# Two-layer hybrid encoder on one core: the products of probabilities and values in two matmuls a block, and one evacuation for two heads

## The chip, the core and the metric

The kernel runs on one core of one Trainium2 chip. The metric is the device time of one execution in microseconds (us). It is compared by the median of several runs; one further execution is taken with the hardware profiler, and its page and trace are what this document reads. Engines are named as in the profile: PE is TensorE (matmuls; PEld are its weight loads), DVE is VectorE, ACT is ScalarE, POOL is GpSimd, and SP issues transfers.

## The reference, cut to what matters

Two layers over 2048 tokens of width 1024. In each layer the normalised input goes through one wide projection; its columns feed a chunked attention (8 heads of 64) and a retention (4 heads of 128); both are gated, joined and projected back onto the input. The change touches the last step of the attention:

```python
def hybrid_layer(x, norm_gain, w_in, w_out, rel_bias, cos, sin):
    hn = rms_norm(x, norm_gain)
    aq, ak, av, ag, rq, rk, rv, rg = jnp.split(hn @ w_in, cuts, axis=-1)
    ya = chunked_rel_attention(aq, ak, av, rel_bias)      # softmax(q k / 8 + bias) v, own chunk + 8 before
    yr = chunkwise_retention(rq, rk, rv, cos, sin)
    y = jnp.concatenate([ya * silu(ag), yr * silu(rg)], axis=-1)
    return x + y @ w_out
```

For each token and head, `ya` is the sum over up to 576 keys of probability times value, where the probabilities are exponentials divided by their sum.

## The kernel before, in words

**Numbers in two halves.** Wherever precision matters, a float32 array is held as two float16 arrays, an upper half (the rounded value) and a lower half (what is left). A product then takes three matmuls: upper by upper, upper by lower, lower by upper.

**Tiles and stages.** Tokens go in 16 tiles of 128, four tiles to a block of 512 (n = 0 to 3). For each layer l and each of four groups s (two attention heads and one retention head), and for each block n, `dense_T` makes queries and keys, `dense_V` makes values and gates, and `attention` runs on the block. The main loop interleaves them: `run` takes one *round* of the dense work (eight matmuls of 512 columns), then lets the deferred work that has come due be issued (`tick`; `later(k, fn)` means: k rounds from now), then takes one step of the attention of the block before. One attention of a block has 24 rounds, six for each tile. After the last group comes `wout`, the projection back.

**Order.** PE, ACT, DVE and POOL issue their instructions in the order in which the program is written; an engine that waits holds up everything behind it on the same engine. SP's transfers have an order of their own except for those marked `in_turn`.

**Attention of a unit** (one tile a, one head hx; L830 to L882). `qk` makes the scores S in PSUM (L845, L846), VectorE adds the bias and takes the maximum (L849, L851), ScalarE makes the exponentials (L852) and their upper half (L854), GpSimd the lower half (L855), and a transposing transfer (L857) puts keys on the partitions: `u.p[:, b]` is the upper and `u.p[:, nb + b]` the lower half of block b of 128 keys, with nb up to 5 blocks. Two units later `pv` (L860) multiplies with the values. The values lie as `st.v[:, a, hx, 0:129]`: 64 columns upper half, one column of ones (L789), and 64 columns lower half (L811). Before, `pv` takes a PSUM bank for each unit and issues three matmuls a block: upper probabilities by upper values and ones (65 columns, L865), upper probabilities by lower values (64 columns, L866, added into the same columns 0 to 63), lower probabilities by upper values and ones (65 columns, L867). Column 64 is the sum of the probabilities. One round later `out_` (L869) takes its reciprocal (L871), multiplies it with the group's scale `g.ka` (L872) and scales the 64 columns with it and with the gate (L877). When both heads of a tile are there, y goes out to memory (L880). With rounds counted in a tile from 0: the first head's `pv` is in round 0, its `out_` at the tick of round 1, the second head's `pv` in round 3 and its `out_` at the tick of round 4.

**Retention** (L909). For each tile, a product r1 in round 0 (L916, masked at L918), and a product r2 in round 5 (L928, L931), evacuated by L939, L951 and L956; `sh` (L907) is the state's half for the next tile.

**PSUM.** Eight banks. Two (psD) hold the dense sums, two (psS) the scores, and four (psR, tag "small") everything else: the unit's o, r1, r2, and the sums of squares of weights that are being prepared (`allsum`, L334). A psR bank that has become free is given to the next taker in the order of last uses in the program.

Of the kernel before, what the change touches and what calls it, by code (L numbers as in the profile page):

```python
# [10 lines left out]
F32 = mybir.dt.float32  # L11
I32 = mybir.dt.int32
AF = mybir.ActivationFunctionType
ALU = mybir.AluOpType
# [4 lines left out]
P = 128  # L19
# [8 lines left out]
def hybrid_trunk(ctx: ExitStack, tc: tile.TileContext, x, pos, gain, gcol, w_in, w_out, rel, fgain,  # L28
# [8 lines left out]
    act, dve, pool, pe, sp = nc.scalar, nc.vector, nc.gpsimd, nc.tensor, nc.sync  # L37
# [5 lines left out]
    b2 = ctx.enter_context(tc.tile_pool(name="b2", bufs=2))  # L43
# [7 lines left out]
    psR = ctx.enter_context(tc.tile_pool(name="psR", bufs=4, space=PSUM))  # L51
# [16 lines left out]
    y_d = [dp.tile([P, D], F32, tag=f"y_d{t}", name=f"y_d{t}") for t in range(NT)]  # L68
# [554 lines left out]
    def in_turn(i):  # L623

        if not ring.get("free"):
            return
        tc.keep_in_program_order(i)


    def flow(k=0):  # L630

        if len(pipe) > k:
            pipe.pop(0)()
# [3 lines left out]
    def later(k, fn):  # L637
        deferred.append([k, fn])
# [184 lines left out]
    def attention(l, s, n, g, st, prev):  # L823
        units = []
        for a in range(4):
            for hx in range(2):
                units.append((a, hx))
        ya = {}

        def qk(a, hx):  # L830

            u = St()
            u.a, u.hx = a, hx
            u.nm = f"{l}_{s}_{n}_{a}_{hx}"
            u.nb = nb = min(5, 4 * n + a + 1)
            u.w = w = nb * P
            u.kts = [(st if t // 4 == n else prev, t % 4) for t in range(4 * n + a + 1 - nb, 4 * n + a + 1)]
            S = psS.tile([P, 1024], F32, tag="S", name=f"S{u.nm}")
            cs = slice(a * P, (a + 1) * P)
            cuts = sorted({0, nb} | {j for j in range(nb) if u.kts[j] == (st, 0) or j == 4})  # L840
            for j0, j1 in zip(cuts, cuts[1:]):
                q_, a_ = u.kts[j0]
                k_ = q_.k[:, hx, a_ * P:(a_ + j1 - j0) * P]
                o = S[:, j0 * P:j1 * P]
                pe.matmul(o, st.q[:, hx, 0, cs], k_, start=True, stop=False)  # L845
                pe.matmul(o, st.q[:, hx, 1, cs], k_, start=False, stop=True)  # L846
            v = b2.tile([P, 640], F32, tag="sc", name=f"sc{u.nm}")[:, 0:w]
            m = b2.tile([P, 1], F32, tag="mq", name=f"mq{u.nm}")
            dve.tensor_tensor_reduce(out=v, in0=S[:, 0:w], in1=g.bias[hx][:, 640 - w:640], scale=1.0, scalar=-3.0e38,  # L849
                                     op0=ALU.add, op1=ALU.max, accum_out=m)  # L850
            dve.tensor_scalar(m, m, g.nc[:, 0:1], LN_PSC, op0=ALU.mult, op1=ALU.add)  # L851
            act.activation(v, v, AF.Exp, bias=m[:, 0:1], scale=g.c[:, 0:1])  # L852
            pq = b2.tile([P, 1280], F16, tag="pq", name=f"pq{u.nm}")
            act.activation(pq[:, 0:w], v, AF.Copy)  # L854
            pool.tensor_tensor(pq[:, w:2 * w], v, pq[:, 0:w], op=ALU.subtract)  # L855
            u.p = b2.tile([P, 10, P], F16, tag="pT", name=f"pT{u.nm}")[:, 0:2 * nb, :]
            later(1, lambda: sp.dma_start_transpose(out=u.p, in_=pq[:, 0:2 * w]))  # L857
            return u

        def pv(u):  # L860
            t = 4 * n + u.a
            o = psR.tile([P, 512], F32, tag="small", name=f"o{u.nm}")
            for b, (q_, a_) in enumerate(u.kts):
                v_ = q_.v[:, a_, u.hx, :]
                pe.matmul(o[:, 0:65], u.p[:, b, :], v_[:, 0:65], start=(b == 0), stop=False)  # L865
                pe.matmul(o[:, 0:64], u.p[:, b, :], v_[:, 65:129], start=False, stop=False)  # L866
                pe.matmul(o[:, 0:65], u.p[:, u.nb + b, :], v_[:, 0:65], start=False, stop=(b == u.nb - 1))  # L867

            def out_():  # L869
                rl = b2.tile([P, 1], F32, tag="rl", name=f"rl{u.nm}")  # L870
                dve.reciprocal(rl, o[:, 64:65])  # L871
                dve.tensor_tensor(rl, rl, g.ka, op=ALU.mult)  # L872
                if u.hx == 0:
                    ya[u.a] = b2.tile([P, P], F32, tag="ya", name=f"ya{u.nm}")
                y = ya[u.a]
                vs = slice(u.hx * 64, u.hx * 64 + 64)
                dve.scalar_tensor_tensor(out=y[:, vs], in0=o[:, 0:64], scalar=rl[:, 0:1], in1=st.g[u.a][:, vs],  # L877
                                         op0=ALU.mult, op1=ALU.mult)
                if u.hx == 1:
                    later(1, lambda: in_turn(sp.dma_start(y_d[t][:, s * P:(s + 1) * P], y)))  # L880

            later(1, out_)  # L882

        ret = retention(l, s, n, g, st)
        rounds_ret = (5, 10, 10, 14, 14, 18, 18, 23) if (l, s, n) == (0, 0, 0) else [6 * a + b for a in range(4) for b in (0, 5)]
        for i, (a, hx) in enumerate(units):
            flow(1)
            u = qk(a, hx)
            for r in range(3 * i, 3 * i + 3):
                for _ in range(rounds_ret.count(r)):  # L890
                    next(ret, None)
                if r % 3 == 2:
                    pipe.append(lambda u=u: pv(u))
                yield
# [319 lines left out]
    def grp(l, s):  # L1214
        if (l, s) not in groups:
            groups[l, s] = Grp()
        return groups[l, s]
# [138 lines left out]
    for j in range(4):  # L1356
        o = VSEC[j] * 512
# [80 lines left out]
    for l in range(DEPTH):  # L1438
        gO = [Grp(), Grp()]
        go = Grp()  # L1440
        for s in range(NSW):
            g = grp(l, s)
            for n in range(NS):
                first = (l, s, n) == (0, 0, 0)
                if not first:
                    st = St()
                    states[l, s, n] = st
                    dT = dense_T(l, s, n, g, st)
                else:
                    st = st0  # L1450
# [129 lines left out]
```

## Time and profile before

| what | before |
|---|---|
| median of 3 runs | 2061.82 us (2058.64 to 2061.86) |
| span of the profiled execution, first to last instruction | 2060.7 us |
| mean granted clock of TensorE | 0.995 |
| ACT busy | 1134.8 us, 55% |
| POOL busy | 688.1 us, 33% |
| instructions | 39339 |

The profiled execution's time is its span and the little that lies before the first and behind the last instruction; the median run is 1.1 us above that span. How to read a row of the groups: line, engine, operation, output<-inputs by the program's names, shapes and count; then the busy time and the mean of one in nanoseconds; then the time that the engine sat idle right before them, and what ended most of it. A row of the timeline is start, duration, engine, line, operation and count; in brackets stands the idle time before it and what released it. In a row of the windows each engine has its busy time and, in parentheses, its instructions. Matmuls overlap one another, so their durations add up to more than the time they take.

### The profile page before, as it was taken

To read this page: it belongs to the slowest core of one execution; us is meant where nothing else is said; L and a number is where in the kernel's file an instruction comes from. 1 tells how busy PE (TensorE), PEld (TensorE's weight loads), DVE (VectorE), ACT (ScalarE), POOL (GpSimd) and SP (SyncE) were. 2 spreads that over 40 slices of the span, in tenths; PEclk is the share of its full clock that TensorE was granted. 3 is DMA by queue.
4 is the path that set the end of the run, shared out by engine and by line. 5 is a ranking of instruction groups with operands and counts; after the bars stand their busy time and mean duration, and the time that the engine had idled before them with its cause. 6 is when DMAs were issued, how large, how long until landed. Compare 5 with 4: busy or idle time off the path is not lost. (4 is left out here: it accounts for less than half of the span.)

```text
span 2060.7 us, 39339 instructions
## 1 busy us (share of the span) xinstructions
PE 1999.4 (97%) x14038; PEld 1052.9 (51%) x14038; DVE 1228.1 (60%) x3804; ACT 1134.8 (55%) x2526; POOL 688.1 (33%) x701
## 2 busy tenths in 40 slices
PE   6988999999999999999999999999999999999998
PEld 4444555555555555554444555555555555555544
DVE  6776666565556555666553556555655566557643
ACT  6556665556565645555444546655656565455432
POOL 0344343434334434430003443444333334333100
PEclk9999999999999999999999999999999999999999
DMA  8778664547584754899774546554746775658864
GB/s 227 169 161 178 155 148 109 112 114 164 117 185 113 165 128 101 174 209 263 219 185 113 124 104 156 116 126 103 158 117 150 148 155 124 129 115 187 224 203 139
DMA packets 645701, 313.64 MB, mean 152 GB/s; under 512 B 459232, under 2 KB 602080, under 8 KB 645504
## 3 DMA queue, kind: packets, MB, share of 16 engines
q1 hardware_dynamic: 645504, 311.12, 65.6%
q8 instruction: 110, 1.80, 0.4%
q14 instruction: 87, 0.71, 0.1%
HBM read 123.26 MB, written 41.98 MB: 80 GB/s over the span
## 5 line engine op out<-in xcount | busy, mean ns | idle before, releaser
L855 POOL TENSOR_TENSOR pq<-sc,pq 128x640 f16<-128x640 f32 (+4 forms) x256 | 319.4, 1248 | 860.5 <-ACT pq L854 443.8
L852 ACT ACTIVATE sc<-sc,mq,cT 128x640 f32<-128x640 f32 (+4 forms) x256 | 218.4, 853 | 615.6 <-DVE rl L871 309.7
L797 PE MATMUL dV<-whV,hTh 128*128 128x512 f16 x1024 | 353.9, 381 | 7.3 <-DVE gt L815 6.1
L797 PE MATMUL dV<-whV,hTl 128*128 128x512 f16 x1024 | 353.8, 381 | 0.0
L797 PE MATMUL dV<-wlV,hTh 128*128 128x512 f16 x1024 | 353.8, 381 | 0.0
L778 PE MATMUL dT<-hTh,whT 128*128 128x512 f16 x1008 | 346.6, 379 | 2.7 <-DVE kk L697 1.3
L778 PE MATMUL dT<-hTl,whT 128*128 128x512 f16 x1008 | 346.6, 379 | 0.0
L778 PE MATMUL dT<-hTh,wlT 128*128 128x512 f16 x1008 | 346.6, 379 | 0.0
L797 PEld LDWEIGHTS <-hTh 128*128 128x128 f16 x2048 | 197.0, 98 | 224.7 <-DVE gt L815 10.0
L778 PEld LDWEIGHTS <-whT 128*128 128x128 f16 x2016 | 192.1, 98 | 207.7 <-issue 1.6
L849 DVE CUSTOM_DVE_ANT_0 sc<-S,bias 128x640 f32<-128x640 f32 (+4 forms) x256 | 188.3, 735 | 88.8 <-PE S L846 87.4
L1172 PE MATMUL dO<-whO,yly 128*128 128x512 f16 x504 | 191.0, 379 | 1.7 <-DMA yly<-hTl 1.1
L1172 PE MATMUL dO<-whO,yhy 128*128 128x512 f16 x504 | 191.0, 379 | 1.0 <-DMA yhy<-hTh 1.0
L1172 PE MATMUL dO<-wlO,yhy 128*128 128x512 f16 x504 | 191.0, 379 | 0.0
L854 ACT ACTIVATE pq<-sc 128x640 f16<-128x640 f32 (+4 forms) x256 | 171.5, 670 | 8.1
L797 PEld LDWEIGHTS <-hTl 128*128 128x128 f16 x1024 | 99.4, 98 | 112.4 <-issue 3.9
L1172 PEld LDWEIGHTS <-yhy 128*128 128x128 f16 x1008 | 98.1, 98 | 113.7 <-DMA yhy<-hTh 1.5
L778 PEld LDWEIGHTS <-wlT 128*128 128x128 f16 x1008 | 97.2, 98 | 113.7 <-issue 6.0
L845 PE MATMUL S<-k,q 128*128 128x128 f16 (+3 forms) x592 | 142.4, 267 | 0.0
L865 PE MATMUL o<-v,pT 128*128 128x65 f16 x1120 | 129.8, 193 | 6.4 <-DMA pT<-pq 5.5
L866 PE MATMUL o<-v,pT 128*128 128x64 f16 x1120 | 130.1, 195 | 0.0
L846 PE MATMUL S<-k,q 128*128 128x128 f16 (+3 forms) x592 | 129.7, 267 | 0.0
(359 smaller groups left out, 3476.5 us busy)
## 6 DMA issues: line engine op xcount, KB each, us to landing
q<-qq SPq DMA_DIRECT2D x128, 128.0 KB, 2.4
yyy<-y_d SPq DMA_DIRECT2D x32, 512.0 KB, 4.5
stT<-in_w_in_dram SPq DMA_DIRECT2D x27, 512.0 KB, 4.8
stV<-in_w_in_dram SPq DMA_DIRECT2D x26, 512.0 KB, 4.6
k<-kk SPq DMA_DIRECT2D x128, 64.0 KB, 2.0
swp<-rot SPq DMA_DIRECT2D x64, 128.0 KB, 3.1
tabc<-tab SPq DMA_DIRECT2D x32, 256.0 KB, 3.0
tabs<-tab SPq DMA_DIRECT2D x32, 256.0 KB, 3.1
```

Source lines behind the costliest of these rows:

```text
L778: pe.matmul(ps, w_[:, j, kt, :], h_[:, kt, :], start=(m == 0), stop=(m == 23))
L797: pe.matmul(ps, h_[:, kt, a * P:(a + 1) * P], w_[:, kt, :], start=(m == 0), stop=(m == 23))
L845: pe.matmul(o, st.q[:, hx, 0, cs], k_, start=True, stop=False)
L846: pe.matmul(o, st.q[:, hx, 1, cs], k_, start=False, stop=True)
L849: dve.tensor_tensor_reduce(out=v, in0=S[:, 0:w], in1=g.bias[hx][:, 640 - w:640], scale=1.0, scalar=-3.0e38, op0=ALU.add, op1=ALU.max, accu ...
L852: act.activation(v, v, AF.Exp, bias=m[:, 0:1], scale=g.c[:, 0:1])
L854: act.activation(pq[:, 0:w], v, AF.Copy)
L855: pool.tensor_tensor(pq[:, w:2 * w], v, pq[:, 0:w], op=ALU.subtract)
L865: pe.matmul(o[:, 0:65], u.p[:, b, :], v_[:, 0:65], start=(b == 0), stop=False)
L866: pe.matmul(o[:, 0:64], u.p[:, b, :], v_[:, 65:129], start=False, stop=False)
L1172: pe.matmul(ps, h_[:, kt, :], w_[:, kt, :], start=(m == 0), stop=(m == 23))
```

## The change

A unit's three matmuls a block become two: the upper probabilities meet all 129 columns of the values at once (upper values, ones, lower values), so that the products with the lower values land in columns 65 to 128 of the bank; the lower probabilities meet the first 65 columns as before. Both heads of a tile share one bank, each in a half of 256 columns, taken at the first head. Nothing is evacuated after the first head. One round after the second head's products, VectorE takes the reciprocal of both sums, copies the columns 65 to 128 of both heads to `y`, adds them to the columns 0 to 63 into unused columns of the same bank, scales that by `g.ka` and the reciprocals, and multiplies with the gates into `y`.

```diff
         def pv(u):
             t = 4 * n + u.a
-            o = psR.tile([P, 512], F32, tag="small", name=f"o{u.nm}")
+            if u.hx == 0:
+                ya[u.a] = psR.tile([P, 2, 256], F32, tag="small", name=f"o{u.nm}")
+            o = ya[u.a]
             for b, (q_, a_) in enumerate(u.kts):
                 v_ = q_.v[:, a_, u.hx, :]
-                pe.matmul(o[:, 0:65], u.p[:, b, :], v_[:, 0:65], start=(b == 0), stop=False)
-                pe.matmul(o[:, 0:64], u.p[:, b, :], v_[:, 65:129], start=False, stop=False)
-                pe.matmul(o[:, 0:65], u.p[:, u.nb + b, :], v_[:, 0:65], start=False, stop=(b == u.nb - 1))
+                pe.matmul(o[:, u.hx, 0:129], u.p[:, b, :], v_, start=(b == 0), stop=False)
+                pe.matmul(o[:, u.hx, 0:65], u.p[:, u.nb + b, :], v_[:, 0:65], start=False, stop=(b == u.nb - 1))
+            if u.hx == 0:
+                return
+            y = b2.tile([P, 2, 64], F32, tag="ya", name=f"ya{u.nm}")
+            rl = b2.tile([P, 2, 1], F32, tag="rl", name=f"rl{u.nm}")
 
             def out_():
-                rl = b2.tile([P, 1], F32, tag="rl", name=f"rl{u.nm}")
-                dve.reciprocal(rl, o[:, 64:65])
-                dve.tensor_tensor(rl, rl, g.ka, op=ALU.mult)
-                if u.hx == 0:
-                    ya[u.a] = b2.tile([P, P], F32, tag="ya", name=f"ya{u.nm}")
-                y = ya[u.a]
-                vs = slice(u.hx * 64, u.hx * 64 + 64)
-                dve.scalar_tensor_tensor(out=y[:, vs], in0=o[:, 0:64], scalar=rl[:, 0:1], in1=st.g[u.a][:, vs],
-                                         op0=ALU.mult, op1=ALU.mult)
-                if u.hx == 1:
-                    later(1, lambda: in_turn(sp.dma_start(y_d[t][:, s * P:(s + 1) * P], y)))
+                w = o[:, :, 192:256]
+                dve.reciprocal(rl, o[:, :, 64:65])
+                dve.tensor_copy(y, o[:, :, 65:129])
+                dve.tensor_tensor(w, y, o[:, :, 0:64], op=ALU.add)
+                dve.scalar_tensor_tensor(out=w, in0=w, scalar=g.ka[:, 0:1], in1=rl.to_broadcast([P, 2, 64]), op0=ALU.mult,
+                                         op1=ALU.mult)
+                dve.tensor_tensor(y, w, st.g[u.a][:, 0:P].rearrange("p (h d) -> p h d", h=2), op=ALU.mult)
+                yf = y.rearrange("p h d -> p (h d)")
+                later(1, lambda: in_turn(sp.dma_start(y_d[t][:, s * P:(s + 1) * P], yf)))
 
             later(1, out_)
```

## The prediction

> **What bounds the kernel now.** I read the page's busy shares first, then the windows by stage, then the matmuls of the changed lines one by one, and last the waits of TensorE, since only those can turn work of VectorE into time.
>
> ```profile
> span 2060.7 us, 39339 instructions
> PE 1999.4 (97%) x14038; PEld 1052.9 (51%) x14038; DVE 1228.1 (60%) x3804; ACT 1134.8 (55%) x2526; POOL 688.1 (33%) x701
> ```
>
> ```profile
> core 0: us, PE busy (x) PEld busy (x) DVE busy (x) ACT busy (x) POOL busy (x), PEclk, DMA share, GB/s
> 80.00:480.00 400.00, 381.50 (x2776) 201.81 (x2775) 250.17 (x816) 237.49 (x543) 151.29 (x148) 0.98 0.64 142
> ...
> 1060.00:1500.00 440.00, 438.47 (x3131) 231.04 (x3129) 247.96 (x827) 241.94 (x572) 162.40 (x163) 1.00 0.56 126
> ```
>
> In the second layer's attention stage, 440 us long, TensorE is busy for 438.47 us, at a granted clock of 1.00; VectorE is busy for 247.96 us. TensorE sets the time, the other engines have room, and a shorter stream of matmuls shortens the span one for one, unless TensorE is made to wait. There is one weight load for each matmul (14038 of both).
>
> The span of the profiled execution is 2060.7 us; the median of the three timed runs is 2061.82, so 1.1 us lie around the span. I make the sum against the span and add 1.1 at the end. The three runs lie between 2058.64 and 2061.86, so I take 0.2% (4.1 us) as the smallest difference that a measurement here tells from none.
>
> **The matmuls.** Per block of 128 keys the three matmuls of L865 to L867 become two. 1120 matmuls and 1120 weight loads go:
>
> ```profile
> L866 PE MATMUL o<-v,pT 128*128 128x64 f16 x1120 | 130.1, 195 | 0.0
> L865 PE MATMUL o<-v,pT 128*128 128x65 f16 x1120 | 129.8, 193 | 6.4 <-DMA pT<-pq 5.5 <-DVE ya L877 0.8
> L867 PE MATMUL o<-v,pT 128*128 128x65 f16 x1120 | 129.2, 193 | 0.0
> ```
>
> It would be wrong to book 1120 times 195 ns (218 us). Those durations overlap; what counts is from one start to the next. The timeline of TensorE shows one unit of five blocks (15 matmuls from the first row to the last row of L867), the scores after it, and a retention product:
>
> ```profile
> 704.60 0.19 PE L865 MATMUL o<-v,pT 128*128 128x65 f16 x1
> ...
> 705.03 0.19 PE L867 MATMUL o<-v,pT 128*128 128x65 f16 x1
> 705.06 0.22 PE L845 MATMUL S<-k,q 128*128 128x128 f16 x1
> 705.12 0.22 PE L846 MATMUL S<-k,q 128*128 128x128 f16 x1
> 705.17 0.33 PE L845 MATMUL S<-k,q 128*128 128x384 f16 x1
> ...
> 705.50 0.22 PE L845 MATMUL S<-k,q 128*128 128x128 f16 x1
> ...
> 705.61 0.33 PE L899 MATMUL r<-rot,rot 128*128 128x128 f16 x3
> 705.78 0.38 PE L797 MATMUL dV<-wlV,hTh 128*128 128x512 f16 x1
> ```
>
> Fifteen matmuls take 705.06 - 704.60 = 0.46 us, 30.7 ns each, 92.0 ns a block. Two of 128 columns take 0.11 us (55 ns each), three of them 0.17 (56.7); I take 56 for 129 columns. Two of 384 columns take 0.33 us, so a column costs (165 - 55) / 256 = 0.43 ns, and the rest of a matmul only 1 to 4 ns. **The columns stay the same:** 65 + 64 + 65 = 194 before, 129 + 65 = 194 after. All that is saved is the small fixed part of one matmul. After, a block takes 56 + 30.6 = 86.6 ns, and the saving is 5.4 ns x 1120 = **6.0 us**. The ends: if 65 columns follow the slope from 128 (56 - 63 x 0.43 = 29), a block takes 85 and 7.8 us are saved; if time goes by columns alone, nothing is saved; and if a 129th column opens a second pass, it costs more (a rival below).
>
> The Trainium skill, "TensorE: Matmul & The Clock Gate", section "Back-to-back issue gap", speaks against the change: it says that a stream in which every matmul has its own weight load runs at about 81 ns a matmul for 128 columns. By that, as an estimate, a block would take 81 + 30.7 = 111.7 ns and the kernel 22 us more. This trace doesn't agree: its 128-column matmuls, each with its load, start 55 to 57 ns apart.
>
> **VectorE.** Before, each unit has a reciprocal, a product and a scaling of 64 columns; after, each pair of units has five instructions of 128 columns (two for the reciprocal). No row is these five; the nearest are the last three here, which read PSUM at the same width or copy one column:
>
> ```profile
> L871 DVE RECIPROCAL rl<-o 128x1 f32<-128x1 f32 x256 | 40.3, 157 | 0.0
> L872 DVE TENSOR_TENSOR rl<-rl,kaV 128x1 f32<-128x1 f32 x256 | 55.8, 218 | 8.9
> L877 DVE SCALAR_TENSOR_TENSOR ya<-o,rl,gt 128x64 f32<-128x64 f32 x256 | 72.7, 284 | 9.7 <-DVE rl L872 0.6
> L918 DVE TENSOR_TENSOR r<-r,msk 128x128 f32<-128x128 f32 x128 | 37.1, 290 | 0.0
> L956 DVE SCALAR_TENSOR_TENSOR yr<-r,rss,gt 128x128 f32<-128x128 f32 x128 | 44.4, 347 | 23.5 <-POOL rss L952 22.5
> L327 DVE CAST mbT<-m1T 128x1 bf16<-128x1 f32 x28 | 4.4, 156 | 44.3 <-ACT whT L320 44.2
> ```
>
> Reciprocal 157; copy between 156 (one column) and 290, I take 290, as it has the columns of L918; sum 290; scaling with a scalar 347; product 290: 1374 ns per tile against 2 x 659 = 1318. Over 128 tiles that is 7 us more on an engine that is idle for 40% of the span: no cost by itself. What matters is that it comes as one piece, twice as long, behind the second head. How VectorE follows on itself:
>
> ```profile
> 714.27 0.21 DVE L851 TENSOR_SCALAR mq<-mq,ncT 128x1 f32<-128x1 f32 x1
> 714.40 0.16 DVE L871 RECIPROCAL rl<-o 128x1 f32<-128x1 f32 x1
> 714.59 0.16 DVE L872 TENSOR_TENSOR rl<-rl,kaV 128x1 f32<-128x1 f32 x1
> 714.78 0.28 DVE L877 SCALAR_TENSOR_TENSOR ya<-o,rl,gt 128x64 f32<-128x64 f32 x1
> ```
>
> An instruction that needs the one before starts 0.03 us after its end (714.40 to 714.59), one that doesn't, before that end (0.13 after the start of a 0.21 one). So the piece was 0.19 + 0.19 + 0.28 = 0.66 us long; it becomes 0.13 + 0.32 + 0.32 + 0.38 + 0.29 = **1.44 us**, 0.78 more after every second head, and 0.58 less after every first. Bounds: 1.2 with a copy of 156, 2.6 if one of its instructions is held as long as the worst L872 (below). Behind it wait the next maximum (L849), the evictions of dense banks, and the bank's next owner.
>
> **The banks.** The pool psR has four. A tile took four of them (o, r1, o, r2) and now takes three, but holds o from the first head's products to the end of the 1.44 us. A free bank goes to the next taker in the program in the order of last uses. Following that order, the bank of o usually goes to r2 of the next tile, about seven rounds after its last read, and r1 and o get banks free for longer: no wait. The exceptions are where a sum of a weight's squares (L334) takes a bank out of turn. Today TensorE waits there already:
>
> ```profile
> 238.98 0.16 PE L334 MATMUL msV<-mbV,ones 128*128 128x1 bf16 x1 [1.22 <-DVE ya L877]
> 239.01 0.38 PE L797 MATMUL dV<-wlV,hTh 128*128 128x512 f16 x1
> 252.91 0.16 PE L334 MATMUL msV<-mbV,ones 128*128 128x1 bf16 x1 [0.70 <-DVE ya L877]
> 267.65 0.16 PE L334 MATMUL msV<-mbV,ones 128*128 128x1 bf16 x1 [1.51 <-DVE ya L877]
> 229.18 0.19 PE L865 MATMUL o<-v,pT 128*128 128x65 f16 x1 [0.81 <-DVE ya L877]
> 107.12 0.22 PE L899 MATMUL r<-sh,rot 128*128 128x128 f16 x1 [1.49 <-DVE sh L907]
> ```
>
> ```profile
> 101.40 0.16 DVE L871 RECIPROCAL rl<-o 128x1 f32<-128x1 f32 x1
> ...
> 102.16 1.28 DVE L1251 SCALAR_TENSOR_TENSOR hTh<-hTh,rsn,gb 128x1024 f32<-128x1024 f32 x1
> ...
> 238.26 0.16 DVE L871 RECIPROCAL rl<-o 128x1 f32<-128x1 f32 x1
> ...
> 238.64 0.28 DVE L877 SCALAR_TENSOR_TENSOR ya<-o,rl,gt 128x64 f32<-128x64 f32 x1
> ```
>
> The first three wait for the piece of a second head (it ends at 238.92, TensorE goes on at 238.98), and their bank is again that of this o: each grows by 0.78, **+2.3 us**. At 107.12 TensorE waits for a chain of VectorE without a gap that has a second head's piece in it at 101.40; its successor, at 102.16, could start at 102.76: **+0.6**. At 229.18 a second head waits to take a bank of its own, which it no longer needs: **-0.8**. The next closest has room:
>
> ```profile
> 1473.53 0.16 DVE L871 RECIPROCAL rl<-o 128x1 f32<-128x1 f32 x1
> ...
> 1475.67 0.17 PE L334 MATMUL msV<-mbV,ones 128*128 128x1 bf16 x1
> ```
>
> 1473.53 + 1.44 leaves 0.70 us; there are five such sums. The freed 0.58 us after first heads I book at nothing: no wait of TensorE has it in its chain. The store of y (L880) is the same transfer, still one round after the second head's piece.
>
> Sum: -6.0 + 2.3 + 0.6 - 0.8 = -3.9; 2060.7 - 3.9 = 2056.8, plus 1.1: **2057.9 us**.
>
> **Rivals.**
> - *More is saved.* The waits at the sums are made up in gaps that follow, and 65 columns follow the slope: up to 7.8 us less, 2054.0. For it: these waits lie in the early stage, where TensorE is busy for 381.50 of 400 us and has gaps to give back. Against: behind a sum the next dense matmul follows at once (239.01).
> - *Columns alone.* The fixed part isn't a matmul's but comes with short ones, and the waits stay: +2.1, 2063.9. Against: two lengths, 65 and 128, give nearly the same small rest. In this case the change doesn't do what it is said to, fewer instructions without less time.
> - *The 129th column opens a second pass* (slower). Its price lies between that of 128 and, by the slope, 256 columns (110 ns): at worst 110 + 30.6 - 92.0 = 48.6 ns x 1120 = 54 us. I price it at one short matmul's 30.7 more: a block takes 117.3, 25.3 more than before, so +28.3, with the waits +30.4, and the kernel takes 2092. It makes the kernel slower by 0.2% from 63 ns on. Against: L866 with 64 columns and L867 with 65 last 195 and 193 ns, so the 65th opened none.
> - *A long matmul waits for its own weight load* (slower). The loads last 1052.9 / 14038 = 75 ns on average. At 75 + 30.7 = 105.7 a block, 13.7 more, the kernel takes 15.3 + 2.1 more, 2079. Against: the 55 ns of the scores, each with its load. The 81 ns of the Trainium skill's page above would be of this kind.
> - *VectorE's piece is held up* (slower):
>
> ```profile
> L872 DVE TENSOR_TENSOR rl<-rl,kaV x256: 158/159/1337, 92.3 to 1938.5; 128x1 f32<-128x1 f32 x128
> L877 DVE SCALAR_TENSOR_TENSOR ya<-o,rl,gt x256: 283/284/286, 92.5 to 1938.7; 128x64 f32<-128x64 f32 x128
> ```
>
> Minimum, median, maximum: L872 is sometimes held for 1.18 us. If two of the new ones were held so each time, the three sums pay 3 x 2.36 and the five others 5 x (2.36 - 0.70): +15.4, 2073.3. It eats the gain from 0.9 us on. Against: L877, with an operand in PSUM, never is (286 at most), and each new instruction but the reciprocal's small output touches PSUM.
>
> **How the numbers follow.** Forecast 0.55 (own range 2055 to 2061), more saved 0.17, columns alone 0.08, second pass 0.08, held up 0.10, weight load 0.02. The forecast lies about on the bound of 0.2% (2057.7), so half of it, 0.27, and the second case make faster 0.44; second pass, weight load, most of held up and some of columns alone make slower 0.21; the same is 0.35. The range 2053 to 2068 leaves out about 0.05 below and 0.15 above.
>
> **What would show it.** Right: L865 with 129 columns 56 ns before the next start, 87 ns a block; 2240 instead of 3360 products; the five instructions within 1.5 us; L334 waiting about 0.8 longer at the same three places, and no other wait behind psR. Wrong: a 129-column spacing over 60 ns, waits of r1, r2 or o for the piece, or a stage of the second layer that shrinks by anything but 5 ns a block.

## The result, and the profile after

| | before | after |
|---|---|---|
| median of 22 runs each | 2059.41 us | 2056.51 us |
| lowest to highest | 2055.88 to 2063.85 | 2051.30 to 2061.46 |
| span of the profiled execution | 2060.7 us | 2056.7 us |
| mean granted clock | 0.995 | 0.993 |

The ratio is 0.9981, with a 95% interval from 0.9974 to 0.9989: 0.19% faster, some 3.9 us, where the forecast was a sum of -3.9. The profiled span, 2056.7, is 0.1 us beside the 2056.8 of the prediction. That is closer than its terms deserve, as the later sections show: several were off and made up for each other. (The execution that the profiler took is 2.4 us above the median before and 2.0 us above it after, so the two spans can be compared.)

The page after, and the same two stages in the view of windows (same columns as before):

```profile
span 2056.7 us, 36849 instructions
PE 1996.4 (97%) x12918; PEld 1048.5 (51%) x12918; DVE 1239.1 (60%) x3676; ACT 1134.8 (55%) x2526; POOL 685.7 (33%) x701
```

```profile
80.00:480.00 400.00, 378.43 (x2513) 199.69 (x2512) 252.36 (x782) 236.29 (x539) 150.60 (x148) 0.98 0.64 141
1060.00:1500.00 440.00, 439.84 (x2897) 231.86 (x2896) 253.03 (x798) 243.89 (x578) 163.01 (x165) 1.00 0.55 126
```

1120 matmuls are gone (14038 to 12918), and the busy time of TensorE fell by only 3.0 us: durations that overlap say nothing of a matmul's worth. In the second layer's stage TensorE stays busy to the brim, 439.84 of 440 us. VectorE is busy for 11.0 us more over the whole span, 7.5 of them in the changed instructions (176.3 against 168.8 us), where 7 had been forecast.

TensorE's view of groups, and the timeline of one unit of five blocks:

```profile
L867 PE MATMUL o<-v,pT 128*128 128x129 f16 x1120 | 133.8, 222 | 5.4 <-DMA pT<-pq 5.4
L868 PE MATMUL o<-v,pT 128*128 128x65 f16 x1120 | 126.8, 194 | 0.0
```

```profile
705.57 0.22 PE L867 MATMUL o<-v,pT 128*128 128x129 f16 x1
705.63 0.19 PE L868 MATMUL o<-v,pT 128*128 128x65 f16 x1
...
705.97 0.19 PE L868 MATMUL o<-v,pT 128*128 128x65 f16 x1
706.00 0.22 PE L845 MATMUL S<-k,q 128*128 128x128 f16 x1
```

Ten matmuls in 0.43 us, 86 ns a block in this unit. A row of the timeline is rounded to 10 ns, so one unit decides little. The mean of the differences between the starts of neighbours, over all rows of each line, does: before 29.7, 33.4 and 29.9 ns for L865, L866 and L867, together 92.9 a block; after 59.0 (129 columns, without four of over 100 ns) and 29.8 (65), together 88.8. A few of these matmuls, the four among them, ran in stretches of 3.4 or 6.8 us in which the trace shows half the clock granted. Without them a block takes 92.3 ns before and 87.9 after, and 87.9 again in a second profile of the changed kernel (below). **A block saves 4.1 ns as counted and 4.4 ns at the full clock, 4.6 to 4.9 us over 1120 blocks.** The 129th column opened no second pass, and the long matmul waits for no load of its own: either would stand in the 59.0.

VectorE's piece behind a second head, in the timeline, and the spread of its instructions in the view of the bank's tile (minimum, median, maximum in ns):

```profile
250.98 0.16 DVE L327 CAST mbV<-m1V 128x1 bf16<-128x1 f32 x1 [2.80 <-ACT whV L320]
251.05 0.16 DVE L876 RECIPROCAL rl<-o 128x2 f32<-128x2 f32 x1
251.13 0.27 DVE L877 COPY ya<-o 128x128 f32<-128x128 f32 x1
251.44 0.29 DVE L878 TENSOR_TENSOR o<-ya,o 128x128 f32<-128x128 f32 x1
251.76 0.36 DVE L879 SCALAR_TENSOR_TENSOR o<-o,kaV,rl 128x128 f32<-128x128 f32 x1
252.16 0.29 DVE L881 TENSOR_TENSOR ya<-o,gt 128x128 f32<-128x128 f32 x1
```

```profile
L877 DVE COPY ya<-o x128: 264/270/273, 101.0 to 1934.5; 128x128 f32<-128x128 f32 x128
L879 DVE SCALAR_TENSOR_TENSOR o<-o,kaV,rl x128: 359/359/360, 101.7 to 1935.1; 128x128 f32<-128x128 f32 x128
```

The piece lasts from 251.05 to 252.45, 1.40 us. None of its 128 occurrences is held up.

TensorE's waits at the places that the prediction named:

```profile
107.69 0.27 PE L902 MATMUL r<-sh,rot 128*128 128x128 f16 x1 [1.96 <-DVE sh L910]
...
238.57 0.16 PE L334 MATMUL msV<-mbV,ones 128*128 128x1 bf16 x1 [1.98 <-DVE ya L881]
...
252.50 0.16 PE L334 MATMUL msV<-mbV,ones 128*128 128x1 bf16 x1 [0.74 <-DVE ya L881]
...
267.39 0.16 PE L334 MATMUL msV<-mbV,ones 128*128 128x1 bf16 x1 [1.70 <-DVE ya L881]
```

The three sums of squares grew by 0.76, 0.04 and 0.19 us, +1.0 together. The chain at 107 grew by 0.47. The wait of a second head for a bank (229.18 before) is gone. No unit's product and no retention product waits for the piece.

**Where the time is won.** Count TensorE's units of pv from 0 to 255 and compare the starts of the same unit after and before. In the first layer nothing is gained: at unit 126 (928 us before), the last but one of that layer, the changed kernel is 1.5 us late. TensorE's named waits between the units 0 and 126 grew from 22.3 to 26.2 us, more than the 2.4 us that the spacing saves there. Between the units 126 and 128, at the border of the layers, 2.6 us are won; the waits there fall from 6.1 to 4.0 us (2.2 in the second profile); what makes them fall was not tried. From unit 128 to 184 (1117 to 1475 us) TensorE has no named wait, before or after. This is the quiet stage: its 240 blocks gain 1.0 us, and 240 x 4.4 ns = 1.06. At the last unit the changed kernel is 3.9 us early. Its second profile (below) is 4.9 us late at unit 126, gains 3.6 at the border and 1.0 in the quiet stage, and ends 3.9 us early as well.

The other stages are less certain than that, because the granted clock drops in a different place in each execution. In the view of windows it is the third number from the end; first before, then after:

```profile
1600.00:1620.00 20.00, 17.91 (x135) 9.50 (x134) 12.38 (x41) 12.43 (x30) 8.12 (x7) 0.91 0.79 191
```

```profile
1600.00:1620.00 20.00, 18.56 (x120) 9.41 (x118) 13.26 (x47) 12.54 (x32) 8.54 (x8) 1.00 0.72 157
1865.00:1885.00 20.00, 18.04 (x105) 8.84 (x104) 12.85 (x42) 11.38 (x28) 5.74 (x6) 0.91 0.98 210
```

Before, the clock is 0.91 over the 20 us from 1600; after, it is 1.00 there and 0.91 in the 20 us from 1865; in the second profile of the changed kernel it is 0.91 in the 20 us from 595. At each of these places the comparison of the starts jumps by some 2 us. So a stage outside the quiet one can't be read to better than some 3 us.

### The profile page after: what moved, and what is told of

It is laid out like the page before. It is cut to its first block, busy times and chain, and to the rows that moved or that the text cites. A ratio compares the mean times of both kernels' runs of the same rounds, so it can differ in the third digit from the quotient of the medians.

```text
span 2056.7 us, 36849 instructions
## 1 busy us (share of the span) xinstructions
PE 1996.4 (97%) x12918; PEld 1048.5 (51%) x12918; DVE 1239.1 (60%) x3676; ACT 1134.8 (55%) x2526; POOL 685.7 (33%) x701
## 5 line engine op out<-in xcount | busy, mean ns | idle before, releaser
L867 PE MATMUL o<-v,pT 128*128 128x129 f16 x1120 | 133.8, 222 | 5.4 <-DMA pT<-pq 5.4
```

The source lines that it names most:

```text
L867: pe.matmul(o[:, u.hx, 0:129], u.p[:, b, :], v_, start=(b == 0), stop=False)
```

## The experiments

The theory: the matmuls save by their spacing, in every block, and the piece of VectorE gives some of it back at the banks. The rivals: the evacuation, not the matmuls, makes the gain (fewer instructions on VectorE, one bank less a tile); the fixed part of a matmul is not what is saved; and the long piece costs nothing.

### The evacuation alone: three matmuls into the new bank

```diff
-                pe.matmul(o[:, u.hx, 0:129], u.p[:, b, :], v_, start=(b == 0), stop=False)
+                pe.matmul(o[:, u.hx, 0:65], u.p[:, b, :], v_[:, 0:65], start=(b == 0), stop=False)
+                pe.matmul(o[:, u.hx, 65:129], u.p[:, b, :], v_[:, 65:129], start=False, stop=False)
```

> The new evacuation alone: the upper probabilities meet the values in two matmuls again (65 and 64 columns, the second into columns 65 to 128), everything else as in the changed kernel. Theory 1 (the gain is the fixed part of 1120 matmuls, the rest costs a little): a block takes about 92 ns between starts again, the waits at the three sums stay, so the time is that of before plus 0 to 2 us. Rival (the gain comes from the shared bank and the new evacuation): about 4 us below before, as in the changed kernel, with a block still 92 ns.

Measured: 2065.76 us, ratio 1.0023 [1.0013, 1.0032], span 2064.0. A block takes 92.6 ns (29.8, 33.4 and 29.5), as before the change. So the evacuation alone makes the kernel slower, by 4.7 us by the ratio, more than expected. In its profile TensorE's named waits (all rows of the view of waits) add to 57.2 us against 53.9 before; the span grew by 3.3 as well. The largest growths are here:

```profile
PE r L903 <- DVE dT L911: 9.3, 12, 1.6
PE o L867 <- DMA pT<-pq: 8.3, 10, 1.4
```

Before, these are 6.8 us in 9 waits and 5.5 us in 9 (here 9.3 in 12 and 8.3 in 10): the retention's product waits for VectorE's rest of `dT`, and the product with the values for the transfer of `pT`. Neither wait is for a bank. The gain of the change is therefore none of the evacuation's.

### The two matmuls alone: bank and evacuation for each unit

```diff
-            if u.hx == 0:
-                ya[u.a] = psR.tile([P, 2, 256], F32, tag="small", name=f"o{u.nm}")
-            o = ya[u.a]
+            o = psR.tile([P, 512], F32, tag="small", name=f"o{u.nm}")
```

with the same five instructions of `out_` on 64 columns behind every unit.

> The two matmuls alone: a bank for each unit as before, evacuated one round later, but with the copy and the sum that the two matmuls need (five instructions of 64 columns a head). Theory 1: a block takes 88 ns as in the changed kernel, 5 us saved; the piece behind the second head is about 1.15 us instead of 0.66, so the three sums wait 0.5 us longer each than before at most: 3 to 5 us below before. Rival (the shared bank is the gain): no gain, or VectorE's added work (about 0.5 us a head) turns it into a loss of some us.

Measured: 2058.85 us, ratio 0.9989 [0.9980, 0.9998], span 2062.5. The spacing is that of the changed kernel (58.9 and 29.4 ns). The profiled execution was the slowest of its 11 runs, 5.4 us above their median, so its span says little. VectorE pays for twice as many small instructions, and the second heads' old wait for a bank is back:

```profile
PE 1997.0 (97%) x12918; PEld 1047.6 (51%) x12918; DVE 1320.6 (64%) x4316; ACT 1134.9 (55%) x2526; POOL 685.4 (33%) x701
```

```profile
PE msV L334 <- DVE ya L880: 4.7, 3, 2.3
...
PE o L865 <- DVE ya L880: 2.1, 3, 1.3
```

The gain is 0.11%, with VectorE busy for 81.5 us more than in the changed kernel. So the matmuls alone win also with the banks as they were, if narrowly; whether they win less than the whole change is not shown, as the intervals overlap.

The quiet stage separates the two parts, since TensorE hardly waits there in any of these kernels (0.2 us at most). This is how much longer than before each kernel takes from unit 128 to unit 184, beside what the spacing alone gives:

| kernel | by the starts | by 240 blocks at the full clock |
|---|---|---|
| changed, first and second profile | -1.0 and -1.0 us | -1.1 us |
| the two matmuls alone | -1.0 us | -1.1 us |
| the evacuation alone | +0.2 us | +0.1 us |
| second matmul cut in two (below) | +4.2 us | +3.9 us |

The gain belongs to the matmuls, and it is as large as their spacing says. The evacuation earns nothing here, and in the run by itself it costs time.

### A longer piece

Copy and sum are repeated twice; the piece then lasts 2.71 us (242.94 to 245.65) instead of 1.40.

```diff
                 dve.tensor_tensor(w, y, o[:, :, 0:64], op=ALU.add)
+                for _ in range(2):
+                    dve.tensor_copy(y, o[:, :, 65:129])
+                    dve.tensor_tensor(w, y, o[:, :, 0:64], op=ALU.add)
```

> The changed kernel with its copy and sum issued three times in place of once: the piece behind the second head grows by four instructions, about 1.24 us, with the same result. By the prediction's count of banks the three sums of squares pay all of it (3.7 us), five more pay what goes beyond their 0.7 us of room (2.7 us), and the chains at 107, 600 and 1605 us up to 1.2 each: 5 to 10 us above the changed kernel, 1 to 6 above before. If VectorE's idle time covers it, nothing: 4 us below before. If the piece were on the path of every tile, 128 x 1.24 = 159 us more.

Measured: 2096.23 us, ratio 1.0171 [1.0157, 1.0186], span 2096.5. That is 39 us over the changed kernel. The count of banks had given 5 to 10, VectorE's idle time none, and a piece on the path of every tile 159. The waits of TensorE:

```profile
PE r L905 <- DVE dT L913: 12.9, 20, 1.6
PE o L867 <- DMA pT<-pq: 10.7, 8, 2.4
PE msV L334 <- DVE ya L884: 9.7, 8, 3.3
PE msT L334 <- DVE mbT L327: 6.7, 6, 1.9
```

The row of `ya` is what the prediction's count of banks gives: three sums, and five others with about 0.6 us each. It grew by 5.3 us. But the other rows, most of the rise of 29.4 us in all named waits, have no bank in them. One of them, with what TensorE, VectorE and ScalarE do there, in three timelines:

```profile
364.82 0.16 PE L334 MATMUL msT<-mbT,ones 128*128 128x1 bf16 x1 [1.94 <-DVE mbT L327]
```

```profile
360.62 0.29 DVE L924 TENSOR_TENSOR r<-r,msk 128x128 f32<-128x128 f32 x1
364.62 0.16 DVE L327 CAST mbT<-m1T 128x1 bf16<-128x1 f32 x1 [3.71 <-ACT whT L320]
```

```profile
361.07 0.81 ACT L852 ACTIVATE sc<-sc,mq,cT 128x512 f32<-128x512 f32 x1 [4.20 <-DVE r L924]
...
363.45 1.04 ACT L320 ACTIVATE whT<-stT 128x1024 f16<-128x1024 f32 x1
```

By the profile VectorE, with a row that ends at 360.91, releases ScalarE's exponentials at 361.07; ScalarE's list, without a gap, reaches the weights' squares (L320) at 363.45; VectorE waits for them until 364.62, and TensorE until 364.82. VectorE is busy for 275.51 of the 400 us from 80 to 480, but in stretches it is the first link of a chain through two engines that ends at TensorE. All named waits add to 82.6 us against the changed kernel's 53.2; some 10 us of the 39 have no name in that view. The mean granted clock is 0.992, against 0.993 and 0.995 in the two profiles of the changed kernel; as an estimate, 0.001 to 0.003 of the span, 2 to 6 us, may be part of them.

### A still shorter matmul

The second matmul is cut into 33 and 32 columns, with the same 194 columns in all: the change undone for the count of matmuls, in another place.

```diff
-                pe.matmul(o[:, u.hx, 0:65], u.p[:, u.nb + b, :], v_[:, 0:65], start=False, stop=(b == u.nb - 1))
+                pe.matmul(o[:, u.hx, 0:33], u.p[:, u.nb + b, :], v_[:, 0:33], start=False, stop=False)
+                pe.matmul(o[:, u.hx, 33:65], u.p[:, u.nb + b, :], v_[:, 33:65], start=False, stop=(b == u.nb - 1))
```

> The changed kernel with its second matmul cut into 33 and 32 columns, so that a block has three matmuls again, two of them very short. If a matmul costs its columns and a small fixed part, the two of 33 and 32 take about 17 ns each, together 34 for 30: 1120 x 4 ns = 4 to 5 us above the changed kernel, about as before. If a matmul has a floor of about 30 ns whatever its columns (which would also make 65 columns take 30), a block grows by 30 ns: 33 us above the changed kernel, and then the price of a short matmul is its floor and not its columns.

Measured: 2077.05 us, ratio 1.0079 [1.0065, 1.0092], span 2076.0. The timeline of one unit:

```profile
705.62 0.22 PE L867 MATMUL o<-v,pT 128*128 128x129 f16 x1
705.68 0.18 PE L868 MATMUL o<-v,pT 128*128 128x33 f16 x1
705.71 0.18 PE L869 MATMUL o<-v,pT 128*128 128x32 f16 x1
...
706.14 0.18 PE L869 MATMUL o<-v,pT 128*128 128x32 f16 x1
706.16 0.27 PE L845 MATMUL S<-k,q 128*128 128x256 f16 x1
```

Fifteen in 0.54 us, against ten in 0.43. Mean spacings: 56.1 ns for 129 columns, 27.0 for 33, 25.2 for 32, together 108.4 ns a block (rounded), 19.6 more than the changed kernel; times 1120 that is 22 us, and 20 were measured. Neither number expected holds: a matmul of half the columns costs nearly as much as one of 65, at a floor of some 25 ns. The 65 columns at 29.8 lie just above it. That is why the change brings little: the matmuls that it joins were long enough to be paid by their columns.

### Aligned value rows

129 columns take 59.0 ns, where 128 of the scores take 55 to 57. Does the odd length of a value row (258 bytes) cost these 3 ns? The rows are set 272 bytes apart; `y` gets one buffer to make room.

```diff
-        st.v = b3.tile([P, 4, 2, 129], F16, tag="v", name=f"v{nm}")
+        st.v = b3.tile([P, 4, 2, 136], F16, tag="v", name=f"v{nm}")
```

> The changed kernel with the values' rows 136 halves apart instead of 129, so that each row's first half starts at a multiple of 16 bytes (to make room, the tile of y has one buffer in place of two). In the changed kernel the matmul of 129 columns takes 59.0 ns to the next start on average: 56 to 58 where its values start at a multiple of 8 bytes or 2 bytes behind it, 59 to 63 where they start 4 or 6 behind. If the start address is the cause, all take 56 to 57: 1120 x 2.5 = 2.8 us below the changed kernel, 6 to 7 below before. If the odd number of columns or the weights are the cause, the average stays at 59 and the time that of the changed kernel.

Measured: 2055.99 us, ratio 0.9977 [0.9968, 0.9985], span 2054.2; spacings 58.7 and 29.4. The theory of the rows' distance falls. The time agrees with the changed kernel's within the intervals. What stays, with both distances, is a dependence on the place of the block in its unit: at the full clock the five blocks take 57.1, 61.7, 55.8, 57.5 and 60.8 ns here, and 57.1, 60.7, 57.9, 58.7 and 58.9 in the changed kernel. Which of the things that go with that place makes it was not tried.

### The matmuls grouped

All matmuls of 129 columns of a unit first, then all of 65 (a second loop over the blocks), in the hope that the 3 ns come from the alternation.

> The changed kernel with a unit's five matmuls of 129 columns issued one behind the other, and then its five of 65. In the changed kernel 129 columns take 59.0 ns to the next start and 65 take 29.8; before a matmul of 33 columns the 129 take 56.0. If the 3 ns are the price of the alternation (65 columns that go back to the row just read), all but one in five go: 1120 x 0.8 x 3 = 2.7 us below the changed kernel, 6.6 below before. If they belong to 129 columns as such, the time is that of the changed kernel.

Measured: 2056.65 us, ratio 0.9979 [0.9970, 0.9989], span 2054.9. The timeline joins rows of one line:

```profile
804.70 0.45 PE L867 MATMUL o<-v,pT 128*128 128x129 f16 x5
804.99 0.32 PE L870 MATMUL o<-v,pT 128*128 128x65 f16 x5
```

Over all units of five blocks 57.5 and 30.7 ns, 88.2 a block. At the full clock it is 87.8 against 87.9 in the changed kernel: the order moves a nanosecond from one matmul to the other and saves nothing. The time shows no difference either.

### An earlier piece

If the piece is what gives time back, it might be issued earlier: right behind the scores that follow the second head's products in the same round, instead of at the tick a round later.

```diff
-            later(1, out_)
+            outs.append(out_)
+            later(1, run_outs)
...
             u = qk(a, hx)
+            run_outs()
```

> The changed kernel with VectorE's piece issued right behind the scores of the same round, in place of one round later, ahead of the conversions that wait for the squares of the weights. If the waits at the three sums come from the piece standing behind such a conversion (VectorE idle for 2.8 us right before it), they go: 4.4 us below the changed kernel. If the piece itself is what holds the engine up, something else waits for it now, and nothing is gained or a few us are lost.

Measured: 2078.59 us, ratio 1.0081 [1.0068, 1.0094], span 2078.5: slower, by 21 us over the changed kernel. At the three sums the waits did shrink, from 4.4 to 3.1 us (0.67, 0.67 and 1.72), so the loss comes from elsewhere. With the value rows aligned as above:

> Both of the last two together. If the two gains are separate they add up: 7 us below the changed kernel, 11 below before. If either has none, the sum is that of the other.

Measured: 2073.08 us, ratio 1.0059 [1.0046, 1.0073], span 2075.5. In the first of the two the waits have moved:

```profile
PE o L872 <- DMA pT<-pq: 15.5, 11, 3.1
PE r L909 <- DVE dT L917: 11.4, 12, 1.6
```

The products wait for their probabilities' transfer, 15.5 us against 5.4 in the changed kernel. All named waits are 17.0 us more than its 53.2, and the span is 21.8 us longer (at a mean granted clock of 0.991). One suspect is the store of `y`, which is moved too and is handed out in turn with other transfers. So once more with the store left in its old round (`later(2, ...)`):

> As the run in which VectorE's piece was issued one round earlier, but with the store of y kept in the round in which the changed kernel has it. If that run's 20 us of loss came from the store, now one round earlier among the transfers that are kept in order (the probabilities' transposes wait 10 us longer in it), they go, and the waits at the three sums too: 2 to 4 us below the changed kernel. If the loss came from the piece standing ahead of other work of VectorE, it stays: 15 to 20 us above the changed kernel.

Measured: 2072.13 us, ratio 1.0051 [1.0037, 1.0065], span 2068.3. About a third of the loss was the store's place. The wait for `pT` stays:

```profile
PE o L872 <- DMA pT<-pq: 14.3, 12, 2.3
```

With the matmuls grouped as well:

> Both of the last two. Separate gains add up: about 6 us below the changed kernel if both hold; else that of the one that holds.

Measured: 2072.69 us, ratio 1.0054 [1.0040, 1.0068], span 2072.0. Nothing more is won. Every one of the four is slower than the kernel before, and 14 to 21 us slower than the changed one, by a move of the piece by one round in VectorE's list. Which of the instructions behind it makes the transfers of `pT` late was not separated.

### The changed kernel again

> The changed kernel itself beside these, for the scatter: 0.9981 of before within 0.1%, 88.8 ns a block, and the same three waits. Where its second profile differs from the first by some us in a stage, such differences between the profiles of other kernels say nothing.

Measured: 2056.41 us, ratio 0.9977 [0.9966, 0.9989], span 2056.8. Its named waits add to 55.7 us, 2.5 more than in the first profile of the same kernel, with the same 4.4 at the three sums. A block takes 58.7 + 29.3 = 88.0 ns, and 87.9 at the full clock as in the first:

```profile
PE r L902 <- DVE dT L910: 8.6, 11, 1.4
PE o L867 <- DMA pT<-pq: 6.9, 7, 2.2
...
PE msV L334 <- DVE ya L881: 4.4, 3, 2.0
```

So a few us between two profiles, in the rows of `dT` and `pT` above all, are no finding. The kernel with the evacuation alone is 8.7 us slower than the changed one by the ratios (0.0042 x 2060). At the full clock (92.6 - 87.9) x 1120 = 5.3 us of that are the matmuls'; its waits, 57.2 against 53.2 and 55.7, hold 1.5 to 4.0 more. Together that is 6.8 to 9.3 us, so nothing beyond the scatter is left over.

## Why the prediction was right, step by step

**The bound: right.** TensorE's spacing sets the time in the second layer's stage, and there the gain is 1.0 us in 240 blocks, as the spacing gives it.

**The matmuls, -6.0: right in kind, too large by 1.1 to 1.4 us.** Two readings were off, both from one unit of one timeline with rows of 10 ns. A block took 92.9 ns (92.3 at the full clock), not 92.0, and takes 88.8 (87.9), not 86.6. The 65 columns were right by about a nanosecond (29.8, or 29.2, for 30.6), the 129 were not: 59.0, or 58.7, for 56. The value was taken from the scores' 128 columns; the matmul with the lower values was slower already before (33.4 ns for 64 columns, beside 29.7 for 65), which a mean over L866 alone would have shown.

**VectorE's piece, 1.44 us: right**, 1.40. The copy takes 270 and not 290 ns, the scaling with two columns of reciprocals 359 and not 347.

**The three sums, +2.3: the booked term that was most off, +1.0.** The growth was booked three times, and it is paid about once. Each of these waits ends behind the same chain: ScalarE's squares (L320), VectorE's L327, the piece, and then TensorE. The rows of L327 at the first two sums, before:

```profile
238.19 0.16 DVE L327 CAST mbV<-m1V 128x1 bf16<-128x1 f32 x1 [2.79 <-ACT whV L320]
...
252.11 0.16 DVE L327 CAST mbV<-m1V 128x1 bf16<-128x1 f32 x1 [2.79 <-ACT whV L320]
```

and the first of them after:

```profile
237.05 0.16 DVE L327 CAST mbV<-m1V 128x1 bf16<-128x1 f32 x1 [2.79 <-ACT whV L320]
```

The chain is 1.14 us earlier than before at the first sum and 1.13 at the second (250.98): the delay of TensorE at the first sum has not reached it. The sums themselves come 0.41, 0.41 and 0.26 us earlier than before (238.57, 252.50, 267.39 against 238.98, 252.91, 267.65). They are pinned to the chain plus the piece. TensorE came 1.17 us early to the first, lost 0.76 there, and so came only 0.45 early to the second (251.76 against 252.21), where there was nothing more to lose but 0.04. For this stretch TensorE is not the pace, and its savings count for nothing until it is over.

**The chain at 107, +0.6: right**, +0.47. **The wait at 229, -0.8: right**, it is gone. **The five sums with room: right**, none of them waits.

**Another sum, at nothing: wrong, +1.0.** The prediction looked for waits of the sums behind a bank, and booked no change at this one:

```profile
350.48 0.17 PE L334 MATMUL msT<-mbT,ones 128*128 128x1 bf16 x1
```

```profile
351.42 0.16 PE L334 MATMUL msT<-mbT,ones 128*128 128x1 bf16 x1 [1.03 <-DVE mbT L327]
```

Before, TensorE did not wait there; after, it waits for VectorE's L327, which starts 1.28 us later than before (351.21 for 349.93) behind ScalarE's squares, at the end of the same kind of chain as in the kernel with the longer piece. In the second profile this wait is 1.27 us, and the kernel with the evacuation alone has it too (1.0). So it isn't chance, and it is as large as the three sums together.

**First heads' 0.58 us at nothing: right here.** Between the first two sums, apart from the wait for the squares that ends the stretch, VectorE waits for ScalarE once, before the change and after it:

```profile
244.61 1.49 DVE L344 SCALAR_TENSOR_TENSOR wlV<-stV,sV,whV 128x1024 f16<-128x1024 f32 x1 [1.36 <-ACT whV L341]
```

```profile
243.48 1.49 DVE L344 SCALAR_TENSOR_TENSOR wlV<-stV,sV,whV 128x1024 f16<-128x1024 f32 x1 [1.95 <-ACT whV L341]
```

It sits idle 0.59 us longer: the time freed behind a first head is waited away there.

**The sum.** With the terms that the prediction named, -4.6 + 1.0 + 0.5 - 0.8 = -3.9 again, from other numbers: the matmuls saved 1.4 us less, the sums cost 1.3 us less. But this list is not complete: the sum at 351 adds 1.0, the retention's waits for `dT` went from 6.8 to 10.3 us (8.6 in the second profile), and other waits fell by as much. With a scatter of some 2.5 us in the waits of one profile, the equality is luck. What the runs show is that gain and cost are a few us each, and the gain the larger.

**The rivals.** *More is saved*: no, for the spacing; the waits at the sums were indeed smaller, though not by gaps that follow. *Columns alone*: no; the same columns in three matmuls cost 3.9 ns a block more (4.8 at the full clock), in other pieces (129, 33, 32) 19.6 more. *Second pass* and *own weight load*: no, at 59.0 ns. The 81 ns a matmul of 128 columns of the Trainium skill, "TensorE: Matmul & The Clock Gate", section "Back-to-back issue gap", don't occur with 129 either; by that rule the kernel would have been 22 us slower. *The piece is held up*: no, not once in 128 tiles. But had it been, its price was far too low. The prediction counted banks only and had a hold-up eat the gain "from 0.9 us on" at 15 us for 2.36; the longer piece costs 39 us for 1.31 more, and of the 29.4 us that its waits grew by, 5.3 are at the banks. The rest is in waits for `dT`, for L327 behind ScalarE, for the transfers of `pT` and in smaller ones, which a count of banks doesn't show.

**The chances.** The result lies next to the bound of 0.2%: by the ratio the gain is 0.11 to 0.26%. With its middle, 0.19%, the kernel is by that bound the same, which had a chance of 0.35, and not faster, which had 0.44; the interval covers both.

## What to carry to other kernels

Joining two matmuls saves only what each has above its columns, so take the spacing from start to start, as a mean over all of its own line, not from a neighbour of like width: where the short one is well above the floor, it is a few nanoseconds. To see so small a gain, look for a stage in which the engine never waits: there three traces agreed to 0.1 us, while whole spans moved by some us. Waits that end behind one chain are paid about once, not once each; and a longer piece on an engine that is 60% busy is cheap only until the chains that begin on it become late, so try its price by lengthening it, not by counting the waits of today.

## What the runs showed of the hardware

- **A floor for short matmuls.** With a weight load each, 33 columns take 27.0 ns from start to start and 32 take 25.2, while 65 take 29.8. The Trainium skill, "TensorE: Matmul & The Clock Gate", gives about 25 ns for 1 to 64 columns in its table of the section "Back-to-back issue gap"; the trace agrees at 32 and 33 columns, but its 64 columns took 33.4 ns.
- **The matmul with the lower values is slower than its columns say.** 64 columns of lower values take 33.4 ns beside 29.7 for 65 of upper values and ones; 129 of both take 59.0 before a matmul of 65, 57.5 in a row of their like, and 56.1 before one of 33. The distance of the rows is not the cause (58.7 with aligned rows). The cause stays open.
- **Five instructions of VectorE on PSUM, from 160 to 359 ns, hardly vary**: the copy by 9 ns over 128 tiles, the scaling by 1 ns, while the product of two SBUF operands before the change (L872, 159 ns in the median) lasted up to 1337 ns. 41 of its 256 rows last more than 200 ns, and each of these ends 12 to 20 ns behind the end of a GpSimd instruction.
- **The granted clock halves for 3.4 us at a time (twice that in places), not in the same place in each execution.** One such stretch makes the mean of 20 us 0.91: from 1600 us before, from 1865 and from 595 in the two profiles of the changed kernel. What starts one is not shown here.
